# RWKV instructions ranked above the attentions', and the last half's output products in three steps of k tiles

## The chip, the cores and the metric

One core of one Trainium2 chip runs the whole program, and the metric is the device time of one execution in microseconds. The kernel before took 3577.41 us (median of 3 runs, 3570.08 to 3585.98).

## The reference

Two blocks run one after the other on 1024 tokens of 1024 features in float32. The first block (a gated mixer with mLSTM and a channel MLP) is not touched by the change. The second has two layers. Each projects the normalised tokens to the inputs of three branches, mixes the branches' outputs with one matrix, and adds a gated projection:

```python
for i in range(2):
    h = rms_norm(x, norm_g[i])
    z_a, z_b, z_c = split_cols(h @ w_in[i], ...)
    y_a = rwkv7_branch(z_a, ...)      # 6 heads, a state carried from token to token
    y_b = dsa_branch(z_b, ...)        # 4 heads, each query attends to its 256 best keys
    y_c = dilated_branch(z_c, ...)    # 6 heads, three windows
    x = x + concatenate([y_a, y_b, y_c]) @ w_out[i]
    gate = sigmoid(rms_norm(x, ple_norm_g[i]) @ ple_w_gate[i])
    x = x + gate * (p[i] @ ple_w_proj[i])
return rms_norm(x, final_norm_g)
```

## The kernel before

**Halves and units.** The second block works on halves of 512 tokens, four row tiles of 128. For layer i and half h it runs `in2(i, h)` (the input products), the RWKV units of three head pairs p (`rwkv`, lines 1548 to 1554), `branches(i, h)` (both attentions) and `out2(i, h)` (the output and gate products). The calls stand in `block2` (lines 1050 to 1068) in the order in2(0,0), branches(0,0), in2(0,1), branches(0,1), out2(0,0), in2(1,0), branches(1,0), out2(0,1), in2(1,1), rwkv(), branches(1,1), out2(1,0), tail2(1,1). An RWKV unit is put off by one call, so that the first stage of one unit stands beside the later stages of the unit before.

**Products.** Every float32 product is made of three matmuls (line 287) of a high and a low part. `chunk` (line 246) loads two k tiles of 256 weight columns as `wf` (256 KB), ScalarE copies the high part `wh` (line 254) and GpSimd subtracts for the low part `wl` (line 255). Each of the three has 3 buffers. A chunk serves 24 matmuls of 256 columns when four row tiles are worked on together and 12 when two are.

**What waits on VectorE.** The input products leave PSUM through `shift` (lines 1138 to 1140, RWKV inputs) and `gate_out` (line 1148). They lie in two banks with the tag `pd`, so products stop when VectorE is late with these. In the second half of a layer the sparse attention needs `choose` (lines 1691 to 1742): it finds the score of the 256th best key by bisection, 31 turns for a pair of row tiles. A turn has four VectorE instructions (lines 1718 to 1721, the first over 640 to 1024 scores) and one on ScalarE (line 1717). The RWKV unit's own VectorE work is products with masks, a 16x16 inverse (lines 1422 to 1469) and its assembly (lines 1403 and 1404).

**Order.** A scheduler writes each engine's queue ahead of the run, by rank. What is traced inside `high_priority(offset)` ranks as if it had been traced that many instructions earlier:

```python
with self.tc.high_priority(offset=1000000):         # line 1081, branches
self.unit, self.rwkv_first = None, 30000            # line 1048
with self.tc.high_priority(offset=self.rwkv_first): # line 1550, rwkv
```

So both attentions go before RWKV, and RWKV before the dense products.

**Outputs.** Each branch writes its output to `yd[i, h]`, eight k tiles of 128 features: RWKV units 0 to 2 (line 1546), dilated 3 to 5 (line 1755), sparse 6 and 7 (line 1689). `mixed` (line 1914) loads a k tile as `yf` and splits it (lines 1893 and 1894). The last half is `tail2` (lines 1938 to 1963): two row tiles are multiplied over all eight k tiles (`mix2`). The other two follow with four banks of their own, k tiles 0 to 5 before the gate products of the first two and 6 and 7 after them. `prep2` transposes (line 363), `end2` makes the gate products, and line 2012 scales the result. All of this takes each weight twice.

Of the kernel before, what the change touches and what calls it, by code (L numbers as in the profile page):

```python
# [19 lines left out]
D = 1024  # L20
# [79 lines left out]
def prep(a):  # L100
# [9 lines left out]
    g = np.zeros((128, 1), np.float32)  # L110
# [12 lines left out]
    w = f["w_in"][0]  # L123
    sl = lambda o, n: w[:, o:o + n]
# [20 lines left out]
    for i in range(2):  # L145
# [14 lines left out]
        wo.append(wgroups(np.concatenate([o[:3], o[5:], o[3:5]]).reshape(D, D), 256))  # L160
# [23 lines left out]
HEADS = (slice(0, 64), slice(64, 128))  # L184

# [11 lines left out]
class K:  # L197
# [824 lines left out]
    def block2(self):  # L1022
# [25 lines left out]
        self.unit, self.rwkv_first = None, 30000  # L1048
# [469 lines left out]
    def rwkv_y(self, i, h, p, py, bv, sg, t0, t1, tag):  # L1518
# [27 lines left out]
        nc.sync.dma_start(self.yd[i, h][p][:, ts], y)  # L1546
# [87 lines left out]
    def dsa_attend(self, i, h, t, acc):  # L1634
# [10 lines left out]
        for p in range(2):  # L1645
# [43 lines left out]
            nc.sync.dma_start(self.yd[i, h][6 + p][:, rows], y)  # L1689
# [54 lines left out]
    def finish(self, i, h, t, o):  # L1744
# [10 lines left out]
        nc.sync.dma_start(self.yd[i, h][3:3 + n, :, rows].rearrange("j p n -> p j n"), g)  # L1755
# [175 lines left out]
    def add2(self, X, g, ps, ss):  # L1931
        sl = slice(g * 256, g * 256 + 256)
        q = self.stage("sq").rearrange("p (t n) -> p t n", t=2)
        for t, x in enumerate(X):
            self.nc.vector.tensor_add(x[:, sl], x[:, sl], ps[:, 256 * t:256 * t + 256])
            self.square(x[:, sl], q[:, t], ss[:, t, g:g + 1])

    def tail2(self, i, h):


        a = self.mix2(i, h, 0, 2)
        w = [self.I["w2o"][i, g] for g in range(4)]
        X, rows, cs, ys = self.rows2(i, h, 2, 2)
        banks = [self.bank(t, n) for t, n in (("ra", 2), ("ra", 2), ("db", 1), ("pc", 1))]
        jobs = [self.tok_jobs(ps, ys, 0) for ps in banks]
        self.mixed(i, h, cs, ys, range(6))
        for j in range(0, 6, 2):
            for g in range(4):
                self.products(self.chunk(w[g], 256, j), [jobs[g]], 0, 7)
        end = self.end2(i, h, *self.prep2(i, h, *a))  # L1950
        for _ in range(4):
            next(end)
        self.mixed(i, h, cs, ys, range(6, 8))
        ss = self.sums()
        for g in range(4):
            self.products(self.chunk(w[g], 256, 6), [jobs[g]], 0, 7)
            self.add2(X, g, banks[g], ss)
        b = self.prep2(i, h, X, rows, cs, ss, "ra")
        for _ in end:
            pass  # L1960
        self.tags = ["pd", "ra"]
        for _ in self.end2(i, h, *b):
            pass
# [70 lines left out]
```

## Time and profile before

| | |
|---|---|
| median of 3 runs | 3577.41 us |
| the profiled execution | 3562.68 us |
| its span, first to last instruction | 3561.0 us |
| mean granted TensorE clock | 0.944 |
| TensorE matmuls busy | 93% |
| VectorE, ScalarE, GpSimd busy | 57%, 46%, 40% |

The second block begins at about 1340 us of the span. The profiled execution is 14.7 us under the median of the runs. Matmuls are pipelined and their ends are modelled, so a busy TensorE still holds pauses; the count of matmuls in a stretch tells more.

### The profile page before, as it was taken

What the parts mean: (1) busy time and instruction counts of PE and PEld (TensorE: products, weight loads), DVE (VectorE), ACT (ScalarE), POOL (GpSimd) and SP (SyncE); (2) the same over time, 40 slices, a digit from 0 to 9 for tenths busy, and PEclk for the clock granted to TensorE, in tenths of its full rate; (3) what the DMA queues carried; (4) which work ended last, traced back from release to release, by engine and by line L of the source; (5) the groups of instructions that cost most, each with busy time, mean ns of one, the idle gap of its engine ahead of it and who ended that gap; (6) DMA issues with size and microseconds to landing.
All of it is one profiled execution on the core that took longest, in us unless ns stands there. A gap on an engine that the chain in (4) does not pass through costs nothing.

```text
span 3561.0 us, 66181 instructions
## 1 busy us (share of the span) xinstructions
PE 3316.2 (93%) x24420; PEld 2830.0 (79%) x24420; DVE 2042.1 (57%) x5855; ACT 1627.9 (46%) x3496; POOL 1418.2 (40%) x1443
## 2 busy tenths in 40 slices
PE   7989998999999997999999889999999899999977
PEld 5968787899889996786777677777878888778876
DVE  6176959111621155358569986443596359987534
ACT  3244333333423343356447654433564347674444
POOL 1333335444654454442343232234332344323355
PEclk9999998999999998998999689989999899889999
DMA  6333362223233334333423142233343333243254
GB/s 226 122 104 118 109 222 75 93 95 96 91 110 95 95 95 121 114 99 108 126 84 101 48 127 63 80 92 112 95 130 99 115 108 103 72 111 85 69 172 142
DMA packets 327460, 384.99 MB, mean 108 GB/s; under 512 B 113888, under 2 KB 189920, under 8 KB 327136
## 3 DMA queue, kind: packets, MB, share of 16 engines
q1 hardware_dynamic: 327136, 380.76, 35.2%
q8 instruction: 192, 3.15, 0.4%
q14 instruction: 132, 1.08, 0.1%
HBM read 319.73 MB, written 60.92 MB: 107 GB/s over the span
## 4 chain that ended last, share of the span: by engine, by line
PE 42%; DVE 11%; DMA 5%; ACT 2%; issue 2%; POOL 1%; SPq 0%; DVEq 0%; ACTq 0%; POOLq 0%
PE pd L287 26%; PE da L1682 1%; PE ra L1319 1%; PE db L1831 1%; PE da L1618 1%; DVE junk L1718 1%; PE da L1657 1%; PE da L1675 1%; POOL wl L255 1%; PE db L1858 1%; DMA wf<-in_w2o_dram 1%; PE da L1656 1%; DMA wf<-in_w2g_dram 1%; DMA zn<-gd 1%; PE pd L363 1%
## 5 line engine op out<-in xcount | busy, mean ns | idle before, releaser
L255 POOL TENSOR_TENSOR wl<-wf,wh 128x512 fp32r<-128x512 f32 x812 | 1081.3, 1334 | 1503.5 <-ACT wh L254 1420.2
L254 ACT ACTIVATE wh<-wf 128x512 fp32r<-128x512 f32 x812 | 508.6, 628 | 942.3 <-PE pd L287 436.2
L287 PE MATMUL pd<-wh,xh 128*128 128x256 f32 x2240 | 659.5, 297 | 21.6 <-ACT raw L567 6.6
L287 PE MATMUL pd<-wh,xl 128*128 128x256 f32 x2240 | 653.0, 292 | 6.9 <-DVE xl L1894 5.8
L287 PE MATMUL pd<-wl,xh 128*128 128x256 f32 x2240 | 651.4, 293 | 6.8 <-POOL wl L255 5.9
L287 PEld LDWEIGHTS pd<-wh,xh 128*128 128x128 f32 x2240 | 435.6, 195 | 41.0 <-issue 9.2
L287 PEld LDWEIGHTS pd<-wl,xh 128*128 128x128 f32 x2240 | 434.8, 195 | 21.3 <-POOL wl L255 9.6
L287 PEld LDWEIGHTS pd<-wh,xl 128*128 128x128 f32 x2240 | 437.3, 195 | 17.8 <-DVE xl L1894 6.6
L287 PE MATMUL pd<-xh,wh 128*128 128x512 f32 x896 | 369.7, 413 | 30.3 <-DVE tg L1148 20.4
L287 PE MATMUL pd<-xl,wh 128*128 128x512 f32 x896 | 360.7, 403 | 0.2 <-DVE xl L371 0.2
L287 PE MATMUL pd<-xh,wl 128*128 128x512 f32 x896 | 348.3, 403 | 0.1
L287 PEld LDWEIGHTS pd<-xh,wh 128*128 128x128 f32 x896 | 173.8, 194 | 75.0 <-DVE tg L1148 21.5
L1717 ACT ACTIVATE junk<-acc,t_nt 128x512 bf16<-128x512 f32 (+2 forms) x186 | 173.5, 933 | 68.7 <-DVE t_nt L1721 46.1
L287 PEld LDWEIGHTS pd<-xh,wl 128*128 128x128 f32 x896 | 172.8, 193 | 38.0 <-POOL wl L255 1.0
L287 PEld LDWEIGHTS pd<-xl,wh 128*128 128x128 f32 x896 | 173.5, 194 | 36.9 <-issue 2.2
L954 DVE CAST hh<-f 128x512 fp32r<-128x512 f32 x64 | 53.9, 842 | 244.7 <-ACT f L951 244.7
L1718 DVE TENSOR_SCALAR_CACHE_REDUCE junk<-acc,t_nt 128x384 bf16<-128x384 f32 (+2 forms) x186 | 162.8, 875 | 3.0
L1499 POOL TENSOR_SCALAR ch_z<-SS,PC 128x64 f32<-128x64 f32 x96 | 62.1, 647 | 162.4 <-DVE SS L1512 93.8
L1625 DVE SCALAR_TENSOR_TENSOR acc<-r,iw,acc 128x512 f32<-128x512 f32 (+3 forms) x140 | 104.3, 746 | 28.3 <-ACT r L1620 25.5
L287 PE MATMUL pd<-wh,hh 128*128 128x256 f32 x384 | 109.0, 284 | 3.3 <-DVE y L923 3.3
L287 PE MATMUL pa<-wl,hh 128*128 128x256 f32 x384 | 108.1, 285 | 4.2 <-POOL wl L255 4.2
L1620 ACT ACTIVATE r<-da 128x512 f32<-128x512 f32 (+3 forms) x160 | 81.2, 519 | 62.8 <-PE da L1618 52.7
(552 smaller groups left out, 7790.3 us busy)
## 6 DMA issues: line engine op xcount, KB each, us to landing
wf<-in_w_dram SPq DMA_DIRECT2D x256, 256.0 KB, 3.1
wf<-in_w2A_dram SPq DMA_DIRECT2D x144, 256.0 KB, 3.3
wf<-in_w2B_dram SPq DMA_DIRECT2D x112, 256.0 KB, 3.2
wf<-in_w_in_dram SPq DMA_DIRECT2D x80, 256.0 KB, 3.2
wf<-in_w2o_dram SPq DMA_DIRECT2D x80, 256.0 KB, 3.4
wf<-in_w2g_dram SPq DMA_DIRECT2D x80, 256.0 KB, 3.2
wa<-in_w_ada_dram SPq DMA_DIRECT2D x32, 512.0 KB, 5.3
X<-x_d SPq DMA_DIRECT2D x20, 512.0 KB, 5.9
```

What stands on the lines that cost most here:

```text
L254: nc.scalar.activation(wh, wf, AF.Copy)
L255: nc.gpsimd.tensor_sub(wl, wf, wh.bitcast(F32))
L287: self.nc.tensor.matmul(out, lhsT, rhs, start=k == first and j == 0 and q == 0, stop=k == last and j == len(bank) - 1 and q == 2)
L363: nc.tensor.transpose(ps[:, t * 128:(t + 1) * 128], x[:, k * 128:(k + 1) * 128], self.ident)
L954: nc.vector.tensor_copy(hh, f)
L1319: nc.tensor.matmul(ps[:, c * 128:(c + 1) * 128], bk[r, 4 * q + c, 64 * e:64 * e + 128], AR[r, 4 * q + c].rearrange("p j t -> p (j t)"), st ...
L1499: nc.gpsimd.tensor_scalar(zs, S_, PC[:, c:c + 1], None, op0=OP.mult)
L1618: nc.tensor.matmul(ps[:, :n], iqT[:, hd], ikT[:, s0:s0 + n], start=True, stop=True)
L1620: nc.scalar.activation(r[:, :n], ps[:, :n], AF.Relu)
L1625: nc.vector.scalar_tensor_tensor(a, r[:, :n], iw[:, hd:hd + 1], a, op0=OP.mult, op1=OP.add)
L1717: nc.scalar.activation(junk1, x1, AF.Sign, scale=-1.0, bias=nt[:, e1], accum_out=s)
L1718: ts(junk0, x0, nt[:, e0], 0.0, op0=OP.is_le, op1=OP.add, accum_out=c0[:, e0])
```

## The change

RWKV's offset becomes 2000000, above the attentions' 1000000. The rows of `w_out`, and with them the k tiles of `yd`, get another order: dilated 0 to 2, RWKV units 0 and 1 in 3 and 4, sparse 5 and 6, RWKV unit 2 in 7. `tail2` takes all four row tiles at once, in three steps of k tiles (0 to 3, 4 and 5, 6 and 7). After each step and each group of 256 columns the sums are added to X in SBUF by `add2`; squares are taken after the last step alone. It uses the two `pd` banks for the four row tiles of a group, and loads each weight once. Lines from `class K` to `tail2` shift by 2.

```diff
-        wo.append(wgroups(np.concatenate([o[:3], o[5:], o[3:5]]).reshape(D, D), 256))
+        wo.append(wgroups(np.concatenate([o[5:], o[:2], o[3:5], o[2:3]]).reshape(D, D), 256))
...
+Y_DIL, Y_RWKV, Y_DSA = 0, (3, 4, 7), 5
...
-        self.unit, self.rwkv_first = None, 30000
+        self.unit, self.rwkv_first = None, 2000000
...
-    def add2(self, X, g, ps, ss):
+    def add2(self, X, g, ps, ss=None):
         sl = slice(g * 256, g * 256 + 256)
-        q = self.stage("sq").rearrange("p (t n) -> p t n", t=2)
+        q = self.stage("sq").rearrange("p (t n) -> p t n", t=2) if ss is not None else None
         for t, x in enumerate(X):
             self.nc.vector.tensor_add(x[:, sl], x[:, sl], ps[:, 256 * t:256 * t + 256])
-            self.square(x[:, sl], q[:, t], ss[:, t, g:g + 1])
+            if ss is not None:
+                self.square(x[:, sl], q[:, t], ss[:, t, g:g + 1])
...
-        a = self.mix2(i, h, 0, 2)
-        w = [self.I["w2o"][i, g] for g in range(4)]
-        X, rows, cs, ys = self.rows2(i, h, 2, 2)
-        banks = [self.bank(t, n) for t, n in (("ra", 2), ("ra", 2), ("db", 1), ("pc", 1))]
-        jobs = [self.tok_jobs(ps, ys, 0) for ps in banks]
-        self.mixed(i, h, cs, ys, range(6))
-        for j in range(0, 6, 2):
-            for g in range(4):
-                self.products(self.chunk(w[g], 256, j), [jobs[g]], 0, 7)
-        end = self.end2(i, h, *self.prep2(i, h, *a))
-        for _ in range(4):
-            next(end)
-        self.mixed(i, h, cs, ys, range(6, 8))
-        ss = self.sums()
-        for g in range(4):
-            self.products(self.chunk(w[g], 256, 6), [jobs[g]], 0, 7)
-            self.add2(X, g, banks[g], ss)
-        b = self.prep2(i, h, X, rows, cs, ss, "ra")
-        for _ in end:
-            pass
+        X, rows, cs, ys = self.rows2(i, h, 0, 4)
+        ss = self.sums()
+        for j0, j1 in ((0, 4), (4, 6), (6, 8)):
+            self.mixed(i, h, cs, ys, range(j0, j1))
+            for g in range(4):
+                banks = [self.bank("pd") for _ in range(2)]
+                for j in range(j0, j1, 2):
+                    self.products(self.chunk(self.I["w2o"][i, g], 256, j),
+                                  [self.tok_jobs(ps, ys, 2 * c) for c, ps in enumerate(banks)], j0, j1 - 1)
+                for c, ps in enumerate(banks):
+                    self.add2(X[2 * c:2 * c + 2], g, ps, ss[:, 2 * c:2 * c + 2] if j1 == 8 else None)
+        a = self.prep2(i, h, X, rows, cs, ss, "ra")
         self.tags = ["pd", "ra"]
-        for _ in self.end2(i, h, *b):
+        for _ in self.end2(i, h, *a):
             pass
```

The counts of products and of RWKV and attention instructions stay the same. On TensorE the two programs are alike for the first 8476 instructions; from there RWKV's stand a little earlier and the attentions' a little later.

**VectorE, second half of layer 0, the last `gate_out`.** Before, at the last `gate_out` (`tg`, the last input products of this half):

```order
L1877 TENSOR_TENSOR d_q<-d_E,d_m 128x24
L1721 SCALAR_TENSOR_TENSOR t_nt<-t_dec,t_nt 128x2
L1878 TENSOR_TENSOR d_M<-d_q 128x8
L1718 TENSOR_SCALAR junk_22527,t_c_22529<-acc_22300,t_nt 128x896
L1879 TENSOR_TENSOR d_M<-d_M,d_q 128x8
L1148 SCALAR_TENSOR_TENSOR tg<-tg,pd 128x512
L1719 TENSOR_SCALAR t_dec<-t_c_22529,t_kb 128x1
```

In the changed kernel, at the same `gate_out` (L1150 there; L1720 to L1723 are the search, L1405 and L1406 RWKV's inverse):

```order
L1720 TENSOR_SCALAR junk_22527,t_c_22529<-acc_22300,t_nt 128x896
L1150 SCALAR_TENSOR_TENSOR tg<-tg,pd 128x512
L1721 TENSOR_SCALAR t_dec<-t_c_22529,t_kb 128x1
L1405 TENSOR_TENSOR T<-T,ra 32x8x32 x2
L1722 TENSOR_SCALAR t_dec<-t_s,t_k_22531 128x1
L1406 TENSOR_TENSOR TT<-TT,ra 128x512
```

This `gate_out` stood 455 VectorE rows behind the last `shift` of the half's second head pair (L1140), and stands 385 rows behind it now. 52 turns of the search lay between the two, and 40 do now; scores of the dilated attention (L1832) are 18 before and 14 now. These now come behind it. Of two assemblies of the inverse that lay between (two L1403 and one L1404 each), one now stands ahead of that `shift` and the other behind the `gate_out`. In the second half of layer 1 the same count is 38 turns before and 36 now, 14 and 12 of L1832.

**SP, the end of the program, from the last half of RWKV's output on.** Before:

```order
L1546 DMA yd_14164<-y 128x256
L251 DMA wf<-in_w2o_dram 128x512 x7
L1918 DMA yf<-yd_14164 128x256 x4
L251 DMA wf<-in_w2o_dram 128x512 x2
L1918 DMA yf<-yd_14164 128x256 x2
L1976 DMA p<-in_pT_dram 128x256 x2
L251 DMA wf<-in_w2o_dram 128x512 x6
L251 DMA wf<-in_w2g_dram 128x512 x4
```

In the changed kernel:

```order
L1912 DMA X<-x_d 128x1024
L1920 DMA yf<-yd_14164 128x512
L1548 DMA yd_14164<-y 128x256
L1920 DMA yf<-yd_14164 128x512
L253 DMA wf<-in_w2o_dram 128x512 x8
L253 DMA wf<-in_w2g_dram 128x512 x4
```

Behind the first of these rows, the last write of RWKV, 59 weight chunks are still to be loaded before and 28 in the changed kernel. On TensorE the last transposes of RWKV's output (L1538, into `pc`) have 800 matmuls behind them before and 829 now: 125 of the first step's, 96 of the second's, 96 of the third's, 32 transposes and 480 gate products.

## Rows read from the trace of the kernel before

**Rows 1.** The page, parts 1 and 2: busy time by engine, granted clock by slice.

```profile
PE 3316.2 (93%) x24420; PEld 2830.0 (79%) x24420; DVE 2042.1 (57%) x5855; ACT 1627.9 (46%) x3496; POOL 1418.2 (40%) x1443
...
PEclk9999998999999998998999689989999899889999
```

**Rows 2.** The windows view: stretch in us, its length, busy time (instructions) by engine.

```profile
core 0: us, PE busy (x) PEld busy (x) DVE busy (x) ACT busy (x) POOL busy (x), PEclk, DMA share, GB/s
...
1891.00:2078.00 187.00, 169.20 (x1267) 134.21 (x1267) 173.33 (x536) 130.28 (x294) 53.58 (x82) 0.83 0.29 79
...
2184.00:2338.00 154.00, 144.45 (x1192) 118.08 (x1190) 78.11 (x228) 74.59 (x166) 36.05 (x34) 0.92 0.26 80
...
2921.00:3157.00 236.00, 226.43 (x1653) 184.93 (x1649) 216.24 (x636) 160.38 (x356) 85.10 (x126) 0.90 0.32 89
3157.00:3252.00 95.00, 93.82 (x752) 78.50 (x750) 78.07 (x222) 50.41 (x129) 37.98 (x31) 0.93 0.39 113
...
3414.00:3550.00 136.00, 110.55 (x801) 101.62 (x800) 44.33 (x110) 67.97 (x167) 82.72 (x64) 0.95 0.48 147
3414.00:3561.00 147.00, 110.93 (x802) 101.79 (x800) 50.65 (x130) 68.88 (x171) 82.72 (x64) 0.93 0.46 143
```

**Rows 3.** Instructions by form in 1891:2078, VectorE: busy us, mean ns; idle before.

```profile
L1718 DVE TENSOR_SCALAR_CACHE_REDUCE junk<-acc,t_nt 128x896 bf16<-128x896 f32 x27 | 30.8, 1142 | 0.5
...
L1721 DVE SCALAR_TENSOR_TENSOR t_nt<-t_dec,t_nt 128x2 int32<-128x2 int32 x52 | 10.9, 209 | 0.9
...
L1719 DVE TENSOR_SCALAR t_dec<-t_c,t_kb 128x1 int32<-128x1 f32 x52 | 10.7, 206 | 0.3
L1832 DVE CUSTOM_DVE_ANT_0 ds<-db,masks 128x256 f32<-128x256 f32 x19 | 7.9, 418 | 1.2 <-PE db L1831 0.8
...
L1404 DVE TENSOR_TENSOR TT<-TT,ra x2: 686/688/690, 1915.5 to 2069.3; 128x512 f32<-128x512 f32 x2
```

**Rows 4.** Single lines: min/median/max ns, first and last start.

```profile
L1148 DVE SCALAR_TENSOR_TENSOR tg<-tg,pd x4: 682/686/689, 2052.2 to 2078.2; 128x512 f32<-128x512 f32 x4
...
L1935 DVE TENSOR_TENSOR X<-X,pd x16: 406/414/422, 2118.9 to 2183.7; 128x256 f32<-128x256 f32 x16
```

**Rows 5.** The low-part split in 700:1100 and 1891:2078; L1625, 1891:2078.

```profile
L255 POOL TENSOR_TENSOR wl<-wf,wh x140: 1280/1293/1823, 701.3 to 1098.6; 128x512 fp32r<-128x512 f32 x140
...
L255 POOL TENSOR_TENSOR wl<-wf,wh x25: 1264/1292/1554, 1890.0 to 2075.5; 128x512 fp32r<-128x512 f32 x25
...
L1625 DVE SCALAR_TENSOR_TENSOR acc<-r,iw,acc 128x512 f32<-128x512 f32 x21 | 16.9, 803 | 0.2 <-ACT r L1620 0.2
```

**Rows 6.** TensorE's timeline near the end (start, us); SP's longest wait in 3410:3561.

```profile
3412.83 0.28 PE L287 MATMUL pd<-wh,xl 128*128 128x256 f32 x1
3412.95 0.28 PE L287 MATMUL pd<-wl,xh 128*128 128x256 f32 x1
3413.83 0.41 PE L1538 MATMUL pc<-ident,yn 128*128 128x128 f32 x2 [0.60 <-DVE yn L1535]
...
3550.10 0.28 PE L287 MATMUL ra<-wl,z 128*128 128x256 f32 x1
...
SPq L251 <- POOL wl L255: 86.7, 56, 6.0
```

**Rows 7.** VectorE's timeline behind the last product.

```profile
3550.49 0.69 DVE L1993 SCALAR_TENSOR_TENSOR gt<-gt,ra 128x512 f32<-128x512 f32 x1 [5.21 <-PE ra L287]
3551.21 0.76 DVE L1997 SCALAR_TENSOR_TENSOR X<-gt,X 128x256 f32<-128x256 f32 x2
...
3555.24 2.74 DVE L2012 SCALAR_TENSOR_TENSOR X<-X,rms_rs,fng 128x512 f32<-128x512 f32 x4
```

**Rows 8.** VectorE's timeline: the first addition into the last half's X.

```profile
3411.93 0.42 DVE L1935 TENSOR_TENSOR X<-X,pd 128x256 f32<-128x256 f32 x1
```

**Rows 9.** SP, 3300:3561: the last outputs of sparse attention and RWKV, first and last issue.

```profile
L1689 SPq DMA_DIRECT2D yd<-ya x4: 319/326/327, 3311.2 to 3389.4; - x4
...
L1546 SPq DMA_DIRECT2D yd<-y x2: 326/326/326, 3386.3 to 3417.2; - x2
```

More of the change, by code (lines that the diff above doesn't have):

```diff
@@ L1545, in rwkv_y @@
         nc.vector.scalar_tensor_tensor(y, y, 0.5, sg[:, ts], op0=OP.mult, op1=OP.mult)
-        nc.sync.dma_start(self.yd[i, h][p][:, ts], y)
+        nc.sync.dma_start(self.yd[i, h][Y_RWKV[p]][:, ts], y)
     def rwkv(self, *unit):
@@ L1688, in dsa_attend @@
             nc.vector.scalar_tensor_tensor(y, po, 0.5, g, op0=OP.mult, op1=OP.mult)
-            nc.sync.dma_start(self.yd[i, h][6 + p][:, rows], y)
+            nc.sync.dma_start(self.yd[i, h][Y_DSA + p][:, rows], y)
     def choose(self, *tiles):
@@ L1754, in finish @@
         nc.vector.scalar_tensor_tensor(g, ps.rearrange("p (j n) -> p j n", j=n), 0.5, g, op0=OP.mult, op1=OP.mult)
-        nc.sync.dma_start(self.yd[i, h][3:3 + n, :, rows].rearrange("j p n -> p j n"), g)
+        nc.sync.dma_start(self.yd[i, h][Y_DIL:Y_DIL + n, :, rows].rearrange("j p n -> p j n"), g)
     def dil(self, i, h):
```

## The prediction

> **What bounds the kernel now.** The page comes first: TensorE's matmuls are busy for 93% of the span, and the clock's row shows slices at 6 to 8 tenths [rows 1]. So TensorE has work nearly always, but not everywhere at its pace. The windows view tells where not [rows 2]. The reader should compare matmuls per microsecond, since busy time is modelled. In 2184:2338 there are 1192 in 154 us, 7.74 per us, at a granted clock of 0.92. In 1891:2078 there are 1267 in 187 us, 6.78 per us, at 0.83, and there VectorE is busy for 173.3 of 187 us. This is the second half of layer 0 with the search for the 256th key. The same half of layer 1, 2921:3157, has 1653 in 236 us, 7.00 per us, with VectorE busy for 216.2. So VectorE bounds these two stretches: TensorE waits for PSUM banks that `shift` and `gate_out` empty late, and gets a lower clock besides. The last `gate_out` of the first stretch starts at 2078.2 [rows 4].
>
> The end is the other place. From RWKV's last transposes at 3413.83 to the last product at 3550.10 there are 136.3 us [rows 6]. In an unbroken run matmuls of 256 columns start 0.12 us apart (3412.83, 3412.95), and 800 of them at that pace take 96 us. The other 40 us go to weights: 64 splits in 136 us [rows 2], 2.13 us for a chunk, and a chunk feeds only 12 matmuls, 1.44 us. SP waited 86.7 us for GpSimd to free a weight buffer [rows 6], so the ring of three buffers sets this pace.
>
> **The change part by part.**
>
> *The ranks, layer 0, second half.* The order shows what now comes behind the last `gate_out`: 12 turns of the search, 4 scores of the dilated attention and an assembly of the inverse. A turn costs 1.142 for the scores, 0.209 for the update and 0.206 each for two small ones [rows 3], 1.76 us. Twelve make 21.2 us, four scores at 0.418 make 1.7, the assembly's large instruction 0.69; its two smaller ones are left out. That is 24 us of VectorE, and since VectorE is the bound there, the input products could end 24 us earlier. TensorE sets a second limit: at 7.74 per us its 1267 matmuls take 164 us, 23 less than now. Nothing is gone: the additions of the output products (2118.9 to 2183.7 [rows 4]) move up likewise, and the 24 us of VectorE fall behind, at the latest into 2184:2338, where VectorE is busy for 78 of 154 us [rows 2]. 102 of 154 still leaves room, and that work covers it; if VectorE ran without pause there, the gain would be paid back in full. Bounds 0 and 23 us. I take 20, near the upper one, because the stretch that receives the work is half empty.
>
> *Layer 1, second half.* Two turns and two scores move: 3.5 + 0.8 = 4.3 us. The stretch behind, 3157:3252, has VectorE busy for 78 of 95 us [rows 2], so less is free. I take 3. The bounds are -3 (all paid back with a later attention) and 23, which this stretch would give at 7.74 per us (1653 matmuls in 213 us). First halves have no stretch where VectorE is so full; their moves I cost at nothing, covered by dense products.
>
> *A rule that speaks against this.* The dense work that moves up needs its weights split on GpSimd beside a full VectorE. In 1891:2078 the split takes 1292 ns in the median and 1554 at most, in the first block 1293 and 1823 [rows 5]: no sign of a fight. The Trainium skill, page "SBUF — State Buffer", section "SBUF: two separate sides", says that VectorE instructions with two SBUF inputs and a GpSimd instruction lock each other out of a shared port for a whole instruction. The trace disagrees in what can be seen of it here.
>
> *The end.* The changed kernel has 829 matmuls behind RWKV's last transposes and 28 chunks to load in place of 59. A chunk feeds 24 matmuls, 2.87 us, over the 2.13 that a chunk takes now, so TensorE becomes the bound: 829 x 0.12 = 99 us. On top come:
> - the turns of the `pd` banks. A group's additions take 2 x 0.414 per bank [rows 4] and the other bank's 12 matmuls last 1.44, so they should hide; I take 0.3 us for each of some 15 groups, 4 us, with bounds 0 and 1.4 (no hiding) each, 21 in all.
> - the waits at the transposes for the last X and the low parts: 3 us, estimated as a few VectorE instructions of 0.4 to 0.7.
> - the close. Before, 10.9 us from 3550.10 to the end of the span. With four row tiles there are four more scalings (2.74 / 4 = 0.69 each, 2.7 us) and one more turn of the gate, 0.69 + 0.76 [rows 7]: 15.1 us.
>
> This makes 121 us against 147 [rows 2], 26 less. What must arrive: SP's queue puts the second step's weights behind the load of RWKV's last output, which waits for its write. The write was issued 3.4 us behind the transposes [rows 6, 9]; the 125 matmuls of the first step that still follow last 15 us, and that covers it. The squares of the first two steps are not taken, so ScalarE gains no work. The first step's second group waits for the first addition into X; X's load decides that, and it is no earlier than before (3411.93 [rows 8]). With 19 matmuls of that group in front, RWKV's last transposes would come 1 to 2 us later than now. Sum of the end: 24 us less, bounds 8 (no turn hides) and 30 (every turn does).
>
> *Sum.* 20 + 3 + 24 = 47 us off the profiled execution's 3562.7, so 3515.7. That execution is 14.7 us under the median of the runs, so in terms of the median 3577.4 - 47 = 3530 us.
>
> **The rivals.**
> - *Only the end gains.* The work moved out of 1891:2078 is paid back in 2184:2338. For it: the same VectorE work follows. Against it: the half-empty stretch. 3577 - 24 = 3553.
> - *Only the ranks gain.* Two banks for four row tiles turn without cover, and the end loses its 21 us of turns and some waits. For it: VectorE also works on RWKV and splits in the first step. Against it: 1.44 us of the other bank. 3577 - 24 = 3553.
> - *Slower: the attention becomes the path.* The search starts later, the sparse attention's chain of small steps then runs without a pause in 2184:2338, and TensorE starves there as it did before. Price: the stretch grows by 24 us, and its 144 us of busy TensorE get the 0.83 clock of the saturated stretch in place of 0.92, 16 us more; the earlier `gate_out` brings nothing, layer 1 loses 3, the end still gains 24. 24 + 16 + 3 - 24 = 19 slower, 3596. It decides once VectorE has no more idle time in that stretch, which needs 76 us more there and not 24. The sparse attention's last output, issued at 3389.4, is 28 us ahead of RWKV's [rows 9], so at the end it has room.
> - *Weights late.* Each of the 25 splits in 1891:2078 waits out one instruction like L1625, 0.8 us [rows 5]: 20 us, the whole term of layer 0. 3549. The Trainium skill's rule above would do this here.
> - *Nothing moves.* The first 8476 TensorE instructions are alike and the rest shift little; bank turns eat the end and layer 0 pays back: 3577.
>
> **How the numbers follow.** My forecast has a chance of 0.62, only the end 0.13, only the ranks 0.07, weights late 0.03, nothing 0.08, slower 0.07. A measurement of this kernel tells about 0.5% from no change, 18 us, so faster means under 3559.5 and slower over 3595.3. My forecast's own bounds run from 5 us of gain (0 - 3 + 8) to 76 (23 + 23 + 30), most of it beyond 18: 0.60 faster, 0.02 same. The two cases at 3553 lie 6 us inside the bound, with runs that spread 8 us to either side: 0.14 faster, 0.06 same. Weights late: 0.02 and 0.01. Nothing: 0.01, 0.06, 0.01. Slower: 0.02 same, 0.05 slower. Sum: 0.77 faster, 0.17 same, 0.06 slower. The range's lower end is 3577 - 76 - 8 = 3493. Its upper end, 3572, takes in both cases at 3553 and most of the forecast's lower bound, and leaves out the slower one and most of nothing.
>
> **What would show it.** Right: the last `gate_out` of layer 0's second half some 20 us earlier against the start of that half, more matmuls per us and a clock above 0.83 there, VectorE busier in the stretch behind with that stretch no longer; behind RWKV's last transposes about 121 us to the end in place of 147, with some 30 splits in it and SP's wait for buffers gone from TensorE's path. Wrong: TensorE waits for L1935 between groups of the end; TensorE waits for the attention in 2184:2338 or its counterpart; RWKV's last output later against the rest.

## The result and the profile after

The changed kernel takes 3491.9 us (median of 4 runs, 3488.8 to 3502.4), the kernel before in the same job 3580.8: a ratio of 0.9761, 95% interval 0.9729 to 0.9793, so 2.4% faster. The forecast was 3530 with a range from 3493; the median lies one microsecond below that range. The direction was right, and the forecast gain of 47 us is about half of the 89 by which the medians differ. The profiled execution's span is 3487.1 us against 3561.0, 73.9 less: the execution that was profiled before the change (3562.7) is faster than all four runs of before in this job, and the stretches below account for the 73.9 alone.

The page of the changed kernel, parts 1 and 2, answers to [rows 1]:

```profile
PE 3272.3 (94%) x24420; PEld 2810.6 (81%) x24420; DVE 2039.1 (58%) x5842; ACT 1597.4 (46%) x3442; POOL 1377.5 (40%) x1407
...
PEclk9999999999999999999999888999999999879999
```

TensorE has the same 24420 matmuls. GpSimd has 36 instructions fewer (the splits of weights that are no longer loaded twice), and no slice of the clock's row is under 7 tenths, where before there was a 6. The windows view of the changed kernel, with the columns of [rows 2]; the first four stretches are the counterparts of 1891:2078, 2184:2338, 2921:3157 and 3157:3252, the last two those of the end:

```profile
1891.00:2045.00 154.00, 141.99 (x947) 113.46 (x946) 142.26 (x435) 106.52 (x242) 56.87 (x76) 0.88 0.31 86
2151.00:2306.00 155.00, 147.95 (x1240) 121.33 (x1240) 86.96 (x255) 72.38 (x162) 40.14 (x39) 0.91 0.26 79
2874.00:3114.00 240.00, 223.07 (x1739) 183.29 (x1734) 216.47 (x611) 153.21 (x342) 91.14 (x124) 0.91 0.32 89
3114.00:3215.00 101.00, 94.07 (x669) 79.08 (x669) 89.62 (x250) 55.06 (x136) 36.91 (x32) 0.89 0.34 99
3374.60:3473.50 98.90, 98.90 (x832) 98.90 (x831) 41.78 (x92) 45.97 (x119) 40.21 (x31) 1.00 0.30 90
3374.60:3487.10 112.50, 99.22 (x833) 99.02 (x831) 51.17 (x117) 47.78 (x127) 40.21 (x31) 0.95 0.31 98
```

Layer 0's saturated stretch shrinks from 187 to 154 us, and VectorE is just as full in it as before (142.26 of 154, 0.92; before 173.3 of 187, 0.93). It does not hold the same work: 947 matmuls against 1267, so 6.15 per us against 6.78. The sign "more matmuls per us" of the prediction did not come in this window; it comes over the whole half, below. The clock in it did rise, from 0.83 to 0.88. The stretch behind it takes 155 us as before, with 1240 matmuls in place of 1192, so nothing was paid back. The end is 112.5 us in place of 147, with 31 splits and TensorE busy without a gap up to the last product.

The last `gate_out` of layer 0's second half, the first additions into X behind it and the split beside the full VectorE ([rows 4, 5] before):

```profile
L1150 DVE SCALAR_TENSOR_TENSOR tg<-tg,pd x4: 667/681/689, 2025.5 to 2045.1; 128x512 f32<-128x512 f32 x4
...
L1937 DVE TENSOR_TENSOR X<-X,pd x16: 405/418/422, 2084.8 to 2141.6; 128x256 f32<-128x256 f32 x16
...
L257 POOL TENSOR_TENSOR wl<-wf,wh x24: 1267/1292/1741, 1899.6 to 2042.1; 128x512 fp32r<-128x512 f32 x24
```

To see where the 73.9 us went, the second block is cut at events that every kernel has: the first `shift` of a half (its last instruction, on VectorE), the last `gate_out` of a half (on VectorE), the last of RWKV's transposes, the end. The lengths are in us of each profiled execution, from the starts of these instructions.

| stretch | before | changed | difference | forecast |
|---|---|---|---|---|
| up to the last `gate_out` of layer 0's first half | 1630.7 | 1639.4 | +8.7 | 0 |
| A: from there to the first `shift` of the second half | 141.4 | 130.2 | -11.2 | 0 |
| B: to the last `gate_out` of layer 0's second half | 306.1 | 275.5 | -30.6 | -20 |
| C: to the first `shift` of layer 1 | 259.9 | 260.8 | +0.9 | 0 |
| D: to the first `shift` of layer 1's second half | 548.2 | 533.5 | -14.7 | 0 |
| E: to its last `gate_out` | 271.2 | 274.7 | +3.5 | -3 |
| F: to RWKV's last transposes | 256.5 | 260.6 | +4.1 | +2 |
| G: to the end of the span | 147.0 | 112.4 | -34.6 | -26 |

So three things gave more than forecast: B, the end, and the first halves, which were costed at nothing. The first row's 8.7 us say little: before, e2 and e9, whose order is the same there, have 1630.7, 1644.8 and 1637.6.

A border moves with the instruction that marks it, so B and C do not hold the same work in both kernels. Their rows of the windows view, before and then changed:

```profile
1772.10:2078.20 306.10, 281.62 (x2038) 225.37 (x2035) 254.48 (x755) 192.96 (x434) 103.09 (x154) 0.89 0.30 83
2078.20:2338.10 259.90, 242.47 (x1900) 198.21 (x1899) 156.10 (x437) 117.18 (x270) 72.75 (x70) 0.91 0.29 89
```

```profile
1769.60:2045.10 275.50, 259.80 (x1900) 209.21 (x1902) 226.25 (x652) 169.28 (x383) 107.16 (x150) 0.93 0.32 90
2045.10:2305.90 260.80, 250.50 (x2052) 206.10 (x2048) 182.29 (x543) 140.91 (x326) 70.96 (x74) 0.91 0.30 91
```

138 matmuls of B have moved behind the border, some 21 us at B's pace of 6.66 per us. The gain is real all the same, since C takes them in without getting longer: B and C together have 566.0 us before and 536.3 now, 29.7 less, at 6.90 per us in B and 7.87 in C in place of 6.66 and 7.31. A gain in B alone is therefore not read as one below; B and C together are. In the same way E, F and G are read together where work crosses their borders: from the first `shift` of layer 1's second half to the end every kernel has 4726 TensorE instructions.

### The profile page after: what moved, and what is told of

Its sections match the earlier page's. It is cut to its first block, busy times and chain, and to the rows that moved or that the text cites. A ratio compares the mean times of both kernels' runs of the same rounds, so it can differ in the third digit from the quotient of the medians.

```text
span 3487.1 us, 65870 instructions
## 1 busy us (share of the span) xinstructions
PE 3272.3 (94%) x24420; PEld 2810.6 (81%) x24420; DVE 2039.1 (58%) x5842; ACT 1597.4 (46%) x3442; POOL 1377.5 (40%) x1407
## 4 chain that ended last, share of the span: by engine, by line
PE 45%; DVE 10%; DMA 4%; ACT 2%; issue 1%; POOL 1%; SPq 0%; DVEq 0%; ACTq 0%; POOLq 0%
PE pd L289 28%; PE da L1684 1%; PE db L1833 1%; PE da L1677 1%; PE ra L1321 1%; PE db L1860 1%; PE da L1620 1%; PE da L1659 1%; DVE acc L1627 1%; PE da L1658 1%; PE pc L1513 1%; DVE junk L1720 1%; PE pc L1508 1%; PE pc L1504 1%; PE pd L365 1%
## 5 line engine op out<-in xcount | busy, mean ns | idle before, releaser
L257 POOL TENSOR_TENSOR wl<-wf,wh 128x512 fp32r<-128x512 f32 x776 | 1039.7, 1342 | 1392.4 <-ACT wh L256 1329.0
L256 ACT ACTIVATE wh<-wf 128x512 fp32r<-128x512 f32 x776 | 486.4, 628 | 911.1 <-PE pd L289 416.9
L289 PE MATMUL pd<-wh,xh 128*128 128x256 f32 x2336 | 688.3, 297 | 27.2 <-DVE X L1937 8.4
L289 PE MATMUL pd<-wh,xl 128*128 128x256 f32 x2336 | 681.7, 293 | 0.3 <-DVE xl L1896 0.3
L289 PE MATMUL pd<-wl,xh 128*128 128x256 f32 x2336 | 678.1, 293 | 2.1 <-POOL wl L257 1.6
L289 PEld LDWEIGHTS pd<-wh,xh 128*128 128x128 f32 x2336 | 457.4, 197 | 44.9 <-issue 13.1
L289 PEld LDWEIGHTS pd<-wh,xl 128*128 128x128 f32 x2336 | 459.5, 197 | 10.4 <-issue 3.6
L289 PEld LDWEIGHTS pd<-wl,xh 128*128 128x128 f32 x2336 | 457.0, 197 | 11.3 <-issue 2.6
L1719 ACT ACTIVATE junk<-acc,t_nt 128x512 bf16<-128x512 f32 (+2 forms) x186 | 173.4, 932 | 66.5 <-DVE t_nt L1723 52.0
L956 DVE CAST hh<-f 128x512 fp32r<-128x512 f32 x64 | 53.9, 843 | 243.9 <-ACT f L953 243.9
L1720 DVE TENSOR_SCALAR_CACHE_REDUCE junk<-acc,t_nt 128x384 bf16<-128x384 f32 (+2 forms) x186 | 162.8, 875 | 3.1
L289 PE MATMUL pb<-wh,hh 128*128 128x256 f32 x384 | 108.6, 283 | 0.9 <-ACT wh L256 0.9
```

Source lines behind the costliest of these rows:

```text
L256: nc.scalar.activation(wh, wf, AF.Copy)
L257: nc.gpsimd.tensor_sub(wl, wf, wh.bitcast(F32))
L289: self.nc.tensor.matmul(out, lhsT, rhs, start=k == first and j == 0 and q == 0, stop=k == last and j == len(bank) - 1 and q == 2)
L956: nc.vector.tensor_copy(hh, f)
L1719: nc.scalar.activation(junk1, x1, AF.Sign, scale=-1.0, bias=nt[:, e1], accum_out=s)
L1720: ts(junk0, x0, nt[:, e0], 0.0, op0=OP.is_le, op1=OP.add, accum_out=c0[:, e0])
```

## Experiments

All twelve runs stand in one table: ratio to before with its interval, and the stretches above in us.

| kernel | ratio | A | B | C | D | E | F | G |
|---|---|---|---|---|---|---|---|---|
| before | 1 | 141.4 | 306.1 | 259.9 | 548.2 | 271.2 | 256.5 | 147.0 |
| changed | 0.9761 (0.9729 to 0.9793) | 130.2 | 275.5 | 260.8 | 533.5 | 274.7 | 260.6 | 112.4 |
| e1, ranks alone | 0.9863 (0.9832 to 0.9893) | 133.4 | 278.0 | 264.7 | 532.5 | 275.6 | 246.5 | 154.5 |
| e2, old rank, new end | 0.9930 (0.9903 to 0.9958) | 148.6 | 307.1 | 257.6 | 549.8 | 272.2 | 264.0 | 105.3 |
| e4, second halves' ranks, new end | 0.9829 (0.9793 to 0.9865) | 135.5 | 286.2 | 253.1 | 546.8 | 271.6 | 262.3 | 108.0 |
| e5, changed, end loads weights twice | 0.9843 (0.9814 to 0.9871) | 132.4 | 272.4 | 262.8 | 532.0 | 277.6 | 256.3 | 141.1 |
| e9, before, fewer search turns | 0.9985 (0.9967 to 1.0004) | 149.9 | 303.3 | 250.0 | 536.8 | 277.2 | 264.0 | 144.6 |
| e10, changed, fewer search turns | 0.9733 (0.9678 to 0.9788) | 132.3 | 276.7 | 257.2 | 540.5 | 270.7 | 262.2 | 108.1 |
| e7, changed, evictions first | 0.9816 (0.9777 to 0.9855) | 134.2 | 281.4 | 259.0 | 549.8 | 269.9 | 259.7 | 117.4 |
| e3, changed, one step | 0.9781 (0.9750 to 0.9812) | 132.2 | 274.0 | 261.8 | 532.8 | 274.9 | 254.2 | 121.5 |
| e11, before, dilated last | 0.9903 (0.9870 to 0.9935) | 132.6 | 277.4 | 275.6 | 536.5 | 270.4 | 264.7 | 143.7 |
| e12, before, dilated first, sparse last | 0.9906 (0.9879 to 0.9934) | 141.3 | 276.0 | 274.3 | 545.2 | 273.6 | 246.1 | 152.3 |
| e6, before, evictions first | 0.9945 (0.9928 to 0.9962) | 137.8 | 299.0 | 266.5 | 538.9 | 277.8 | 255.8 | 150.9 |
| e13, changed, two steps | 0.9769 (0.9734 to 0.9803) | 132.3 | 272.4 | 262.8 | 534.9 | 275.3 | 254.5 | 115.2 |

How far a stretch repeats is seen where programs are alike. Before and e2 have the same order on TensorE past E (four rows apart): B to E agree within 2.3 us, but A is 141.4 in one and 148.6 in the other. The changed kernel, e1, e5, e3 and e13 are alike up to E: B within 5.6 us, D within 2.9.

### The two parts by themselves

e1 is the kernel before with the rank alone, e2 the changed kernel without it.

```diff
-        self.unit, self.rwkv_first = None, 30000
+        self.unit, self.rwkv_first = None, 2000000
```

> The ranks alone, with the end as before. Theory (the two parts are separate): RWKV's last transposes come 39 us earlier, as in the changed kernel, and the end takes its old 147 us, so about 39 us less than before, ratio 0.989. Rival (the ranks pay only with the new end, since the attention then ends later and the old end waits for it): 15 us less or nothing, ratio 0.996 to 1.0.

> The new order of k tiles and the new end, with RWKV's old rank. Theory: RWKV's last transposes come when they came before and the end takes 112 us in place of 147, so 35 us less, ratio 0.990. Rival (the end gains only because RWKV's higher rank brings the first k tiles early): 15 us less at most, ratio over 0.995.

Measured: the rank alone gives 1.4%, the end alone 0.7%, together 2.4%, so the parts add up within their intervals. The rank's part is in A, in B and C together, and in D; e1's G is even 7.5 us longer than before. The end's part, F and G together since work moves across that border, is 403.5 us before, 401.0 in e1, 369.3 in e2 and 373.0 in the changed kernel: 30 us.

### First halves at the old rank

```diff
+        first = self.rwkv_first if not unit or unit[1] == 1 else 30000
-        with self.tc.high_priority(offset=self.rwkv_first):
+        with self.tc.high_priority(offset=first):
```

> The changed kernel, but RWKV calls of first halves keep the old rank. Theory (the rank pays wherever RWKV stands beside an attention): the first halves lose their gains of the trace, about 10 us in layer 0 and 15 us in layer 1, so about 3517 us, ratio 0.982. Rival (only the search in second halves matters, and the rest came by chance of the execution): as the changed kernel, 3492 us, ratio 0.976.

Measured: 0.9829. B and C together are 539.3 us, nearly the changed kernel's 536.3 (566.0 before), so layer 0's gain needs only the rank of its own half. D falls back to 546.8 from 533.5. The forecast had costed the first halves' moves at nothing; here they are worth 13 us.

### Weights twice

The end keeps its order and three steps, but each chunk is loaded and split once for each pair of row tiles, and feeds 12 matmuls, as before the change.

```diff
-                    self.products(self.chunk(self.I["w2o"][i, g], 256, j),
-                                  [self.tok_jobs(ps, ys, 2 * c) for c, ps in enumerate(banks)], j0, j1 - 1)
+                    for c, ps in enumerate(banks):
+                        self.products(self.chunk(self.I["w2o"][i, g], 256, j), [self.tok_jobs(ps, ys, 2 * c)], j0, j1 - 1)
```

(and the same for the gate products)

> The changed kernel, but in the end each chunk of weights is loaded and split twice, once for each pair of row tiles, so that a chunk feeds 12 matmuls again. Theory (the old end was bound by the pace of weights, 2.13 us a chunk): the stretch behind RWKV's last transposes goes from 112 back to about 140 to 147 us, so about 3520 to 3527 us, ratio 0.983 to 0.985. Rival (the end gains by the steps and the order of k tiles): at most 8 us more than the changed kernel, 3500 us, ratio 0.978.

Measured: G goes from 112.4 to 141.1 us, and F and G from 373.0 to 397.4: 24 of the end's 30 us come back. The windows view of G up to the last product, and what TensorE waited for in all of G:

```profile
3379.50:3507.00 127.50, 112.04 (x849) 104.72 (x849) 46.02 (x97) 66.94 (x153) 85.03 (x65) 0.98 0.50 153
```

```profile
PE pd L289 <- ACT wh L256: 8.8, 13, 1.2
...
PE pd L289 <- POOL wl L257: 3.8, 6, 0.9
```

65 splits in 127.5 us are 1.96 us a chunk, near the 2.13 of before, and TensorE is busy for 112 of 127.5 us, waiting again for weights' high and low parts. So the pace of the weights bounded the old end, and that each is loaded once is what the end gains.

### Less work for VectorE

The prediction's step for layer 0 was that VectorE's work ahead of the last `gate_out` sets stretch B. In e9 the old order stays and work is taken out.

```diff
-        for b in range(30, -1, -1):
+        for b in range(30, last, -1):
```

(`last` is 17 in both searches of layer 0's second half, in e10 11 in the second one alone, else -1)

> The kernel before, with the old ranks and the old end; both searches of layer 0's second half make 18 of their 31 bisection turns (the last 13 are left out, so the kept keys are not exactly the best 256). With each row of VectorE's order priced at its mean duration in the trace of before, the work between that half's first shift and its last gate_out is 294 us before, 263 here and 259 in the changed kernel. Theory (VectorE's work ahead of the last gate_out sets that stretch, and the rank only moves some of it behind): the stretch falls from 306 us to 275 to 280, as in the changed kernel (275.5), the granted clock in it rises, the next half starts about 30 us sooner in the span, and the total is 3545 to 3550, ratio 0.991 to 0.993. Rival (the rank gains because RWKV's own chain of small steps ends sooner, not because there is less VectorE work in front): the stretch stays over 295 us and the ratio over 0.996.

> The changed kernel; the second search of layer 0's second half makes 19 of its 31 turns (the last 12 are left out, so the kept keys are not exactly the best 256). They lie behind the last gate_out there: the priced VectorE work from it to the next half's first shift falls from 216 to 195 us, while the work ahead of it stays at 259. Theory (the stretch behind is TensorE's, with room on VectorE, so what the rank moved there is covered): that stretch stays at 256 to 264 us (260.8 in the changed kernel) and the total within 6 us of the changed kernel's 3492. Rival (part of the gain is paid back there): the stretch falls by 8 to 20 us and the total to 3472 to 3484.

Measured: the theory falls in e9. The waits of TensorE for the banks `db` (dilated attention) and `pd` in stretch B before, then e9's windows view and waits for `db`:

```profile
PE db L1858 <- DVE d_ml L1832: 5.2, 2, 3.8
PE db L1811 <- issue: 2.5, 1, 2.5
PE db L1831 <- DVE d_ml L1832: 2.3, 2, 1.2
PE pd L287 <- DVE tg L1148: 2.0, 1, 2.0
...
PE pd L287 <- DVE prev L1140: 0.7, 2, 0.4
```

```profile
1787.50:2090.80 303.30, 275.75 (x1964) 221.28 (x1960) 231.40 (x623) 159.94 (x365) 102.62 (x153) 0.90 0.29 83
```

```profile
PE db L1858 <- DVE d_ml L1832: 6.5, 3, 5.0
PE db L1831 <- DVE d_ml L1832: 3.9, 3, 2.4
```

VectorE is busy for 23 us less than before, the stretch is 2.8 us shorter though it holds 74 matmuls fewer, and the granted clock is 0.90 in place of 0.89. B and C together are 12.7 us shorter, for 52 us less of VectorE's work in them (the searches end sooner in C); the run as a whole can't be told from before (0.9985). TensorE waits 2.7 us for the `pd` banks of `gate_out` and `shift` in the whole of B before (one row of 2.0 and one of 0.7), so evictions that come late were never a large wait. It waits longer at the matmuls of the dilated attention (L1831, L1858), whose masked scores (L1832) come late; TensorE's matmuls keep their written order whatever they wait for (before and e2 above), so those behind wait too. e10 bears out the other half of the step: of the work behind the last `gate_out`, VectorE lost 20 us (182.29 busy in C of the changed kernel, 161.90 here) and C only 3.6. What the rank puts there is covered. e10's total and the changed kernel's can't be told apart.

### Evictions first

`shift` and `gate_out` are ranked above all else, in e7 in the changed kernel (offset 3000000), in e6 in the one before (2000000).

```diff
+        with self.tc.high_priority(offset=3000000):
             nc.scalar.activation(t, ps, AF.Tanh, scale=0.5)
             nc.vector.scalar_tensor_tensor(t, t, 1.0, ps, op0=OP.add, op1=OP.mult)
```

(for the four instructions of `shift` in the same way)

> The changed kernel with shift and gate_out ranked above RWKV and the attentions as well. Priced VectorE work ahead of the last gate_out falls in layer 0's second half from 259 to 249 us, in layer 1's from 264 to 257, in the first halves from 150 to 140 and from 156 to 147. Theory (VectorE's work in front sets the second halves only): 9 to 11 us less in layer 0's second half (275.5 to about 265), 5 to 7 in layer 1's (274.7 to 268), nothing in the first halves; total 3475 to 3480, ratio to before 0.972 to 0.974. Rival (with the ranks of the change TensorE has become the limit there): nothing, 3488 to 3496. Second rival (the evictions now interrupt RWKV's chains, which are late instead): 5 to 15 us slower than the changed kernel.

> The kernel before with shift and gate_out, the instructions that empty the pd banks of the input products, ranked above both attentions; all else as before. The prediction's step says that TensorE waits in the second halves for banks emptied late. If so, the stretch of layer 0's second half falls from 306 us by 15 or more. By the run with fewer turns, TensorE is held up elsewhere in its queue: then the stretch stays at 300 to 308 us, and the ratio lies between 0.997 and 1.003.

Measured: e7 has less VectorE work ahead of the last `gate_out` (219.2 us busy in B, 226.3 in the changed kernel) and its B is 6 us longer, but holds 2031 matmuls in place of 1900. B and C together are 540.4 us against 536.3, and D is 16 us longer; with 0.9816 it is no better than the change and probably worse. e6 has B at 299.0, and B and C together at 565.5, as before (566.0):

```profile
1762.20:2061.10 298.90, 272.63 (x1987) 219.02 (x1985) 253.06 (x742) 188.51 (x425) 106.96 (x154) 0.90 0.30 84
```

```profile
PE db L1860 <- DVE d_ml L1834: 7.4, 4, 5.0
PE db L1833 <- DVE d_ml L1834: 2.3, 2, 1.7
```

Its waits at the dilated attention are unchanged. That its total is still 0.55% shorter comes, in the profiled execution, from other stretches (A, D and the first half ahead of A).

### Which attention must stand behind

```diff
-                for _ in range(n):
-                    next(blocks, None)
+                with self.tc.high_priority(offset=-980000):
+                    for _ in range(n):
+                        next(blocks, None)
```

(e11, the dilated attention below RWKV; e12 has offset 2000000 there and RWKV's at 2000000, so dilated first, sparse last)

> The kernel before with only the dilated attention ranked below RWKV; the sparse attention with its search stays above it, RWKV's rank and the end are the old ones. Leaving out 36 half turns of the search took 31 us of VectorE's work from in front of the last gate_out of layer 0's second half and the stretch lost 3 us, not 30, so the amount of that work does not set it. New theory (TensorE's in-order queue stands at the dilated attention's matmuls, whose masked scores on VectorE stand behind search turns of the same rank): without the dilated attention in front, that half's stretch from first shift to last gate_out falls from 306 us to 275 to 285 and the waits of TensorE for the dilated scores, 7.5 us there before, fall under 3; total 3525 to 3550, ratio 0.986 to 0.992. Rival (RWKV's chain has to come before the search): the stretch stays over 298 us, ratio over 0.996. Third (any work moved behind gives its own TensorE time alone): 306 less some 7 us.

> The kernel before with the dilated attention ranked first, RWKV second and the sparse attention with its search last; the end is the old one. Theory (the dilated scores must not stand behind search turns; ranked ahead of them they don't either): the stretch of layer 0's second half falls from 306 us to 275 to 285, TensorE's waits for the dilated scores under 3 us; ratio 0.986 to 0.992. Rival 1 (the dilated attention itself has to go behind): over 298 us here while the run with the dilated attention last gains. Rival 2 (RWKV has to come before the search): 270 to 280 us here while the run with the dilated attention last does not gain.

Measured, stretch B of e11 and of e12, with the waits at the dilated attention (in e12 only one of 0.3 us is left):

```profile
1768.50:2045.90 277.40, 261.13 (x1872) 211.20 (x1870) 217.92 (x637) 163.71 (x370) 110.97 (x165) 0.93 0.34 97
```

```profile
PE db L1832 <- DVE d_ml L1833: 2.4, 2, 1.6
...
PE db L1859 <- DVE d_ml L1833: 0.8, 1, 0.8
```

```profile
1782.80:2058.80 276.00, 262.72 (x1858) 213.12 (x1858) 223.00 (x632) 162.92 (x376) 103.52 (x151) 0.91 0.31 88
```

Both bring B down to what the change has, as the new theory has it. But B holds 1872 and 1858 matmuls in them, 166 and 180 fewer than before, and the work that moved lies in C: C is 275.6 and 274.3 where the changed kernel has 260.8. B and C together are 553.0 and 550.3, 13 and 16 us less than before, about half of the change's 29.7. So taking apart the dilated attention and the search, on either side of RWKV, gives about half; the gains of 23 to 30 us came only in orders with both of them behind RWKV (the changed kernel, e1 and e4).

B and C together hold nearly the same TensorE work in all kernels. What the time consists of can be read: the sum of all rows of TensorE's waits, and what the clock takes, estimated as length x (1 - granted clock) of the windows.

| kernel | B + C | TensorE instructions | waits | clock |
|---|---|---|---|---|
| before | 566.0 | 3934 | 41.2 | 57.1 |
| changed | 536.3 | 3946 | 25.0 | 42.8 |
| e4 | 539.3 | 3944 | 27.6 | 43.5 |
| e1 | 542.7 | 3946 | 25.8 | 51.4 |
| e12 | 550.3 | 3934 | 28.6 | 57.8 |
| e11 | 553.0 | 3963 | 31.5 | 49.7 |
| e9 | 553.3 | 3934 | 38.3 | 42.8 |
| e6 | 565.5 | 3931 | 44.4 | 53.9 |

For the changed kernel that is 16.2 us of waits and 14.3 of clock, 30.5 of the 29.7 gained; for the others it comes within 5 us too. So the change's gain is TensorE's own pauses and the lower clock that it was granted. It follows the order more than the amount of VectorE's work: e9, with the old order and 52 us less of that work, gets 12.7 us, nearly all of it clock (its waits are 38.3 us, before 41.2). In every kernel with B under 290 us TensorE waits for the banks `db` 6.2 us or less there, in those over 298 it is 10.9 to 11.9. That these very waits carry the gain is not shown, and two runs speak against their being all of it: e12 waits for `db` only 1.5 us in B and C, as little as the change, and gets half of the gain; e9 waits longer than before, 12.8 us, and gets 12.7. Which of TensorE's waits the order shortens, and why, stays open.

### How many steps the end needs

```diff
-        for j0, j1 in ((0, 4), (4, 6), (6, 8)):
+        for j0, j1 in ((0, 8),):
```

(e13: `((0, 6), (6, 8))`)

> The changed kernel with the last half's output products in one step of all eight k tiles in place of three: each weight is still loaded once for four row tiles, each bank is added to X once and not three times. 835 TensorE instructions stand behind RWKV's last transposes, 830 in the changed kernel. Theory (the end's gain is the weights' being loaded once; the steps only keep TensorE supplied while RWKV's last output travels): from the last transposes to the end 115 to 122 us in place of 112, since TensorE waits 3 to 8 us for that output's way through memory, and the 6.3 us wait for X's first addition ahead of the transposes is gone; total within 8 us of the changed kernel's 3492. Rival (the three steps carry the gain, since without them most output products wait for the last k tile): the end takes over 130 us, total over 3505.

> The changed kernel with the last half's output products in two steps, k tiles 0 to 5 and 6 and 7, in place of three. 835 TensorE instructions stand behind RWKV's last transposes, 227 of them of the first step. Theory (in the changed kernel TensorE stands 6.3 us ahead of the last transposes because the first step's second group needs the first addition into X, whose load comes late; the run with one step had no such wait, but stood behind the transposes until RWKV's last output was back): with two steps the addition into X comes behind the transposes and the first step's products cover that output's way, so from the last gate_out of layer 1 to the last transposes 254 us as with one step (260.6 in the changed kernel), and from there to the end 835 x 0.12 + 13.5 = 114 us (112.4): 4 to 6 us less than the changed kernel, 3485 to 3490, ratio 0.974 to 0.976. Rival (the wait only moves behind the transposes): the end takes 118 us or more and the total is the changed kernel's, 3490 to 3496.

Measured: one step gives 0.9781, two 0.9769; neither can be told from the change's three. The waits of TensorE for the end's products from 3340 us on, in the changed kernel, with one step and with two:

```profile
PE pd L289 <- DVE X L1937: 6.3, 1, 6.3
PE pd L289 <- ACT xh L1895: 1.3, 1, 1.3
```

```profile
PE pd L289 <- ACT xh L1895: 10.3, 4, 5.1
```

```profile
PE pd L289 <- ACT xh L1895: 7.2, 1, 7.2
PE pd L289 <- DVE X L1937: 0.7, 1, 0.7
```

The wait for X's first addition goes, and another for a k tile that is still on its way through memory takes its place; F is 6 us shorter in both, G 3 to 9 longer. The two stretches came out as expected for two steps (254.5 and 115.2), but since a 7.2 us wait came in place of the 6.3, that shorter F isn't shown to be that wait's going. The three steps are not what the end gains; the weights loaded once are. No version tried is measurably faster than the change.

## Why the prediction was right in direction and short in size

- **The ranks, layer 0, second half: right place, wrong mechanism.** The step that failed is "since VectorE is the bound there, the input products could end 24 us earlier". The last `gate_out` did come 30.6 us earlier against the start of the half, and the stretch behind had room, as forecast. But part of that is 138 matmuls that moved behind it, and taking 23 us of VectorE's work away gives 2.8 us (e9), evicting first gives 7 there and nothing with C (e6). A full engine beside a waiting one was read as cause and effect. The waits view of B would have told: 2.7 us at `pd`, 10 at the dilated attention's matmuls. What the runs show in its place is 29.7 us over B and C, which 16.2 us of TensorE's waits and an estimated 14.3 of clock account for, and which follows the order of RWKV against the attentions; why that order saves these waits stays open. That 20 was forecast and 29.7 came is near by luck, since the step that gave the 20 does not hold.
- **First halves at nothing: wrong.** D gave 14.7 us and A 11.2. For D, five kernels with the change's order lie at 532.0 to 534.9, before and e2 at 548.2 and 549.8, and e4 gives the gain back. TensorE's waits there fall only from 31.2 to 27.2 us. Other orders of the same 4128 instructions lie anywhere from 536.5 to 549.8, some from edits that don't touch this stretch (e9, 536.8). So the gain is that order's; that a rank above the attentions must give it isn't shown. A depends on the clock too (below).
- **Layer 1, second half: sign wrong.** Three us of gain were forecast, and E is 3.5 us longer. Five kernels with that order lie at 274.7 to 277.6, before and e2 at 271.2 and 272.2. But E then holds 1876 matmuls in place of 1826, so its length alone is no loss. Over E to G, with equal work, e1 has 676.6 us against 674.7 before, and the changed kernel 647.7 against e2's 641.5: the ranks gain nothing there, and lose 2 to 6 us.
- **The end: right mechanism, size off.** The term was 121 us for G and it measured 112.4. 829 matmuls at 0.12 us were to take 99 us, and from the transposes to the last product there are 99.0:

```profile
3370.51 0.58 PE L289 MATMUL pd<-wh,xh 128*128 128x256 f32 x1 [6.27 <-DVE X L1937]
3370.89 0.41 PE L289 MATMUL pd<-wh,xl 128*128 128x256 f32 x1
3371.10 0.41 PE L289 MATMUL pd<-wl,xh 128*128 128x256 f32 x1
...
3374.58 0.38 PE L1540 MATMUL pc<-ident,yn 128*128 128x128 f32 x2
...
3473.54 0.27 PE L289 MATMUL ra<-wl,z 128*128 128x256 f32 x1
```

  So the turns of the `pd` banks (4 us in the sum) and the waits at the transposes (3) cost nothing: the other bank's 12 matmuls cover a group's additions, as the lower bound had it. The close, 15.1 us in the sum, took 13.5 (VectorE's timeline behind the last product):

```profile
3473.92 0.69 DVE L1988 SCALAR_TENSOR_TENSOR gt<-gt,ra 128x512 f32<-128x512 f32 x1
3474.64 0.76 DVE L1992 SCALAR_TENSOR_TENSOR X<-gt,X 128x256 f32<-128x256 f32 x2
...
3478.69 5.39 DVE L2007 SCALAR_TENSOR_TENSOR X<-X,rms_rs,fng 128x512 f32<-128x512 f32 x8
```

  Eight scalings take 5.39 us, as estimated; no further turn of the gate had to be waited for. The wait for X's first addition was named ([rows 8]) and priced at 1 to 2 us; it is 6.27, and F got 4.1 longer.
- **SP's wait for weight buffers** is still there, 66.5 us in place of 86.7, and now off TensorE's path, since TensorE is busy without a gap:

```profile
SPq L253 <- POOL wl L257: 66.5, 27, 4.4
```

- **Weights beside a full VectorE: small, as forecast, but the trace was misread.** The split takes 1292 ns in the median and 1741 at most beside a VectorE that is busy for 142 of 154 us, so the rival's 20 us did not come. "The trace disagrees" went by the splits' median. The conflict does show, already in the kernel before, on VectorE. L1997 (both inputs in SBUF) takes 409 to 1526 ns, with a GpSimd split beside each one over 1000; L1935 (same shape, one input in PSUM) never takes more than 423. And this L1625, whose median is 744 in 1891:2078, started during a split and ended just after it:

```profile
L1997 DVE SCALAR_TENSOR_TENSOR X<-gt,X x64: 409/424/1526, 2224.1 to 3551.6; 128x256 f32<-128x256 f32 x64
...
L1935 DVE TENSOR_TENSOR X<-X,pd x56: 396/414/423, 2118.9 to 3429.7; 128x256 f32<-128x256 f32 x56
```

```profile
1917.92 1.28 POOL L255 TENSOR_TENSOR wl<-wf,wh 128x512 fp32r<-128x512 f32 x1
...
1918.09 1.67 DVE L1625 SCALAR_TENSOR_TENSOR acc<-r,iw,acc 128x512 f32<-128x512 f32 x1
```

  In the changed kernel six of the 24 splits in 1891:2045 take 1445 to 1741 ns, each begun while a VectorE instruction ran, 1.6 us in all beyond 1292. The Trainium skill, page "SBUF — State Buffer", section "SBUF: two separate sides", has a VectorE instruction with two SBUF inputs and a GpSimd one wait for each other at a shared port; this trace agrees with it.
- **None of the rivals came.** The attention did not become the path, C paid nothing back, and both parts gained.

## What to carry to other kernels

A busy engine next to a waiting one is not yet its cause: before pricing work that moves off a full engine, read in the waits view which bank the waiting engine really stands at, and sum all its waits in the stretch. A stretch that is cut at an instruction which itself moves does not hold the same work in two kernels: count its matmuls before its length is compared. A shorter wait can bring clock with it (16.2 us of waits went with 14.3 of clock here), but need not: e12 has 12.6 us less of waits in B and C and no more clock than before. A weight that is loaded twice because too few rows are worked on together costs whatever the ring's pace is over the matmuls' pace, and sharing the load recovers nearly all of it.

## What was not expected of the hardware

The same program can get a different clock in a stretch. Before, e2 and e9 have the same instructions in the same order in A; it took 141.4, 148.6 and 149.9 us at granted clocks of 0.87, 0.80 and 0.77. The rows of before, of e2 and of e9:

```profile
1630.70:1772.10 141.40, 130.30 (x1013) 102.26 (x1012) 92.45 (x371) 77.02 (x214) 41.85 (x60) 0.87 0.41 118
```

```profile
1644.80:1793.40 148.60, 139.76 (x1013) 109.71 (x1013) 93.62 (x370) 77.49 (x215) 41.75 (x60) 0.80 0.39 113
```

```profile
1637.60:1787.50 149.90, 143.50 (x1014) 112.09 (x1012) 93.24 (x370) 77.49 (x215) 41.75 (x60) 0.77 0.38 112
```

So A's 11.2 us is no fixed price: the profiled execution of before was, at 0.87, the lucky one of the three, and against the other two the changed kernel's 130.2 would be 18 to 20 us less. After a pause the clock costs more: TensorE stood for 6.27 us ahead of 3370.51, and the matmuls of 256 columns behind it start 0.21 us apart up to 3374.4, where they start 0.12 apart in an unbroken run [rows 6]. The windows view of these 4 us and of what follows:

```profile
3370.50:3374.50 4.00, 4.00 (x19) 4.00 (x20) 1.82 (x4) 0.63 (x1) 0.00 (x0) 0.52 0.82 278
3374.50:3384.00 9.50, 9.50 (x81) 9.50 (x81) 4.41 (x10) 4.75 (x9) 3.01 (x3) 1.00 0.33 97
```

At a granted clock of 0.52, the lower of the two levels (1.2 and 2.4 GHz) nearly throughout, 19 matmuls started in 4 us; 0.09 us more for each make some 2 us that this pause cost beyond its own length.
